# A hybrid S5, sliding-window and PEER block on one core: the table stages with all five engines in the order of the text

## The chip, the cores and the metric

The kernel runs on one core of a Trainium2 chip. The metric is the device time of one execution in microseconds. The core has TensorE (PE), VectorE (DVE), ScalarE (ACT) and GpSimd (POOL), and SyncE (SP), which issues loads. ScalarE issues DMAs too, in its own instruction order. Each engine works its instructions off in the order in which the program holds them and waits for others at semaphores, so that order is the thing that this change is about.

## The reference, cut

A decoder block of 512 tokens and width 1024: an S5 branch and a sliding-window attention branch, merged by gates, then the PEER mixer, a retrieval of single-neuron experts by product keys. All in float32. The mixer is the part that the change touches:

```python
def peer_mixer(xn, w_query, sub_keys, u_tab, v_tab):
    q = (xt @ w_query).reshape(t, PEER_HEADS, 2, PEER_KEY_DIM // 2)
    s = jnp.einsum('thkd,hknd->thkn', q, sub_keys)
    vals, idx = lax.top_k(s, PEER_TOPK)
    cand = vals[:, :, 0, :, None] + vals[:, :, 1, None, :]
    best, pos = lax.top_k(cand.reshape(t, PEER_HEADS, -1), PEER_TOPK)
    expert = i1 * N_SUB_KEYS + i2            # 8 heads x 16 of 16384 experts per token
    gate = jax.nn.softmax(best, axis=-1)
    def block_fn(args):
        a = jnp.einsum('cd,ced->ce', xb, u_tab[eb])
        w = gb * jax.nn.gelu(a, approximate=False)
        return jnp.einsum('ce,ced->cd', w, v_tab[eb])
```

## The kernel before

The first 128 tokens go through the mixer by gathering their experts' rows (`sparse`: an indirect load by GpSimd, L1192, and a multiply-add on VectorE, L1209 for a row of the u table and L1211 for one of the v table). The other 384 tokens go through it densely: all 16384 experts are multiplied, with a gate that is zero for those not chosen. The two tables are read in 128 units of 128 experts each.

A **u-unit** computes A = gelu(u . x) of its 128 experts for 384 tokens. Its table rows are loaded by SP (`t_raw`, L1124), split into a rounded part `hi` (ScalarE, L124) and the rest `lo` (VectorE, L125), and multiplied in 24 matmuls (L94 to L96, `pa`); ScalarE takes the gelu (L1136). The result stays on the chip (`A_first`, `A_mid`) or goes to DRAM by a store on ScalarE's queue (`u_g` to `A_d`, L1361). A **v-unit** loads its table rows (L1126), splits them likewise, loads A again if it was stored (`v_a`, L1345, SP) and the gates of eight units at a time (`v_g` from `G_d`, L1141, SP, in four parts), multiplies the two (`v_w`, VectorE L1149), splits the product into `v_wh` (ScalarE, L89) and `v_wl` (VectorE, L90) and adds 18 matmuls of 512 columns to the output (L1160, L1161, L1163, `po`).

The work runs in one list of 256 units, `order`: 96 u-units alone (**stage A**), then the other 32 u-units woven among the 128 v-units (**stage V**). In stage A a background generator, `early()`, is advanced by a credit per unit. It does the top-k (VectorE, L964 to L972, with number copies on ScalarE, L1004) and writes the gates as dense matrices: for each of 48 groups of 8 tokens VectorE builds two one-hot matrices and multiplies in the gates, ScalarE copies the first into another layout (`g_one`, L1108), TensorE multiplies the two (`pg`, L1092 and L1093) and ScalarE evicts the result in two pieces (`g_st`, L1095); every second group its queue stores them to DRAM (`G_d`, L1097). The product of a group is written in the text behind the next group's VectorE work:

```python
nc.vector.tensor_tensor(o1, self.iota16, wide(iT[:, 0, :]), op=ALU.is_equal)   # L1107, g_o
nc.scalar.copy(one, o1.rearrange("p b t -> p t b"))                            # L1108, g_one
nc.vector.tensor_tensor(ol, self.iota16, wide(iT[:, 1, :]), op=ALU.is_equal)   # L1109
nc.vector.tensor_mul(oh, ol, wide(gh))                                         # L1110, g_oh
nc.vector.tensor_mul(ol, ol, wide(gl))                                         # L1111, g_ol
if late:
    multiply(*late)                                                            # pg, g_st, G_d
late = (t1, one, oh, ol)
```

A step i of the loop under `manual_schedule` (L1328) writes, in this order: the table load of unit i+6 (five `t_raw` buffers), the split of unit i+2 (three `hi` and three `lo` buffers), in stage V the loads of `v_g` (five to eight ahead) and `v_a` (four ahead) and the preparation of `v_w` (two ahead); then the matmuls of unit i, with the gelu and the store of A; then the background work and some sparse rows. Engines named in `manual_schedule` keep that order of the text. The others are placed by a scheduler, which puts an instruction where it reckons that its operands are ready. Before, VectorE and GpSimd are named; TensorE, ScalarE and SP are placed by the scheduler. DMAs of SP and of ScalarE's queue share eight completion semaphores, given out in turn in the order of the schedule, and a DMA waits for the one before it on its semaphore.

Of the kernel before, what the change touches and what calls it, by code (L numbers as in the profile page):

```python
# [31 lines left out]
def run_some(gen, credit, add):  # L32

    credit += add
    while credit > 0:
        c = next(gen, None)
        if c is None:
            return 0.0
        credit -= c
    return credit  # L40
# [18 lines left out]
class Builder:  # L59
# [1155 lines left out]
    def run(self, out):  # L1215
        tc, nc, I, L = self.tc, self.nc, self.i, self.pool
        PS = bass.MemoryType.PSUM
        ET = mybir.EngineType
        NB, DT = 128, T - 128
        with ExitStack() as fs:  # L1220
# [104 lines left out]
            def ahead(i, n):  # L1325
                return order[i + n] if 0 <= i + n < len(order) else (2, 0)

            with tc.manual_schedule(engines={ET.DVE, ET.Pool}):  # L1328
                for i in range(-self.FAR, len(order)):
                    v, b = ahead(i, self.FAR)  # L1330
                    if v < 2:
                        raws[v, b] = self.table_load(v * NB + b)
                    if ahead(i, 2)[0] < 2:
                        parts[ahead(i, 2)] = self.unit_split(raws.pop(ahead(i, 2)))
                    if vp:
                        for part in range(self.PARTS):
                            v, b = ahead(i, 8 - part)
                            if v == 1 and b % self.GB == 0:
                                if part == 0:
                                    gg[b] = vp.tile([128, Gd.shape[0], self.GB, self.TS], F32, tag="v_g", name=self.nm("v_g"), bufs=2)  # L1340
                                self.g_load(gg[b], b, Gd, part)
                        v, b = ahead(i, 4)
                        if v == 1 and b not in as_:
                            as_[b] = vp.tile([128, DT], F32, tag="v_a", name=self.nm("v_a"), bufs=4)
                            nc.sync.dma_start(out=as_[b], in_=Ad[b])  # L1345
                        v, b = ahead(i, 2)
                        if v == 1:
                            ws[b] = self.w_prep(vp, as_.pop(b), gg[b - b % self.GB][:, :, b % self.GB, :])
                            if b in homes:
                                free.append(homes.pop(b))  # L1350
                    if i < 0:
                        continue
                    v, b = order[i]
                    if v == 0:
                        kept = bool(free)
                        dst = free.pop(0) if kept else self.wb.tile([128, DT], F32, tag="u_g", name=self.nm("u_g"), bufs=2)
                        self.a_mm(parts.pop((0, b)), xh[:, :, 128:], xl[:, :, 128:], dst)
                        if kept:
                            as_[b] = homes[b] = dst
                        else:  # L1360
                            nc.scalar.dma_start(out=Ad[b], in_=dst)  # L1361
                    else:
                        if b == NB - self.END:
                            for _ in sparse:
                                pass
                        if b == NB - 1:
                            fo = [self.wb.tile([128, D], F32, tag="raw", name=self.nm("fo"), bufs=self.WB[0])
                                  for j in range(DT // 128)]
                            for j, o in enumerate(fo):
                                nc.scalar.dma_start(out=o, in_=hd[j + 1])  # L1370
                        self.v_mm(parts.pop((1, b)), ws.pop(b), po, b == 0, b == NB - 1)
                    if not vp:
                        t_bg = run_some(bg, t_bg, self.RATE_A)
                        if i == self.ALONE - 10:
                            for _ in bg:
                                pass
                    if i >= 4 and self.ready:
                        t_sp = run_some(sparse, t_sp, self.RATE_V if vp else self.RATE_S)
                    if not vp and self.done:
                        rs.close()  # L1380
                        gs.close()
                        pv = L(fs, "pv", space=PS)
                        po = [[pv.tile([128, 512], F32, name=f"po{j}{i}") for i in range(2)] for j in range(DT // 128)]
                        vp = L(fs, "vp", side="right")
                for j in range(DT // 128):
                    for i in range(2):
                        c = slice(512 * i, 512 * i + 512)
                        nc.vector.tensor_add(fo[j][:, c], fo[j][:, c], po[j][i])
                        (nc.scalar if i else nc.sync).dma_start(out=out[j + 1][:, c], in_=fo[j][:, c])
# [77 lines left out]
```

## Time and profile before

| | |
|---|---|
| time, median of 3 runs | 1727.51 us (1727.5 to 1727.69) |
| the profiled execution | 1727.21 us |
| its span in the profile | 1725.4 us |
| mean granted TensorE clock | 0.983 |
| TensorE, VectorE, ScalarE, GpSimd busy | 1625.8, 1426.2, 844.4, 571.4 us |

Times in the profile are microseconds from the start of the span. Busy time is the time in which an engine worked on instructions; "idle before" is its idle time just ahead of an instruction, and the arrow behind it names what it waited for, found from semaphores. "issue" means that nothing was waited for that the profile shows. SPq and ACTq are the queues in which SP and ScalarE issue DMAs. A trailing x3 counts instructions that were put into one row. An instruction's row may begin a little ahead of the end of the one before it, since the engines overlap neighbours; a step is therefore read from start to start. The granted clock is TensorE's, as a share of full speed.

### The profile page before, as it was taken

How to read it: one execution, taken by the hardware profiler on the slowest of the kernel's cores; microseconds unless marked ns; L12 is line 12 of the kernel's file. 1: busy time of each engine (PE TensorE's matmuls, PEld its weight loads, DVE VectorE, ACT ScalarE, POOL GpSimd, SP SyncE). 2: the span in 40 equal slices, each digit the busy share in tenths (PEclk: the TensorE clock that was granted, in tenths of full speed). 3: DMA queues.
4: the chain of work that ended last, by engine and by line, in shares of the span. 5: the costliest groups of instructions: out<-in, count | busy, mean ns of one | idle time of the engine just before them, and what ended most of it. 6: DMA issues, size and time to landing. Idle time of an engine off the chain costs nothing.

```text
span 1725.4 us, 25152 instructions
## 1 busy us (share of the span) xinstructions
PE 1625.8 (94%) x8831; PEld 1429.5 (83%) x8831; DVE 1426.2 (83%) x2931; ACT 844.4 (49%) x1290; POOL 571.4 (33%) x472
## 2 busy tenths in 40 slices
PE   7789999998999899899899889999999999999998
PEld 5568877776899898898899888888888888888876
DVE  7799768897797999999999647877777777777876
ACT  5256565565564457667778423333333333333332
POOL 2563023332521232222222223334434343333441
PEclk9899999999999999999999989999999999999999
DMA  7823452656754567767678987889989989998874
GB/s 230 151 86 99 142 170 74 180 161 185 237 149 164 207 221 281 261 243 272 247 270 325 360 290 270 315 308 330 356 310 338 342 316 340 338 334 311 301 274 171
DMA packets 236302, 429.61 MB, mean 249 GB/s; under 512 B 17376, under 2 KB 153104, under 8 KB 233104
## 3 DMA queue, kind: packets, MB, share of 16 engines
q1 hardware_dynamic: 174464, 240.73, 42.4%
q0 software_dynamic: 36864, 134.23, 21.5%
q10 hardware_dynamic: 24848, 53.06, 9.5%
q8 instruction: 69, 1.13, 0.3%
q14 instruction: 57, 0.47, 0.1%
HBM read 373.69 MB, written 54.26 MB: 248 GB/s over the span
## 4 chain that ended last, share of the span: by engine, by line
PE 60%; DVE 18%; DMA 3%; ACT 3%; issue 3%; POOL 0%; SPq 0%; DVEq 0%; ACTq 0%; POOLq 0%
PE po L1160 10%; PE po L1161 10%; PE po L1163 10%; PE pa L94 7%; PE pa L96 7%; PE pa L95 6%; DVE lo L125 4%; DVE sp_row L1209 2%; ACT hi L124 1%; DVE g_oh L1110 1%; DVE t_s L966 1%; DMA gl<-g_d 1%; DVE g_o L1107 1%; DVE g_ol L1109 1%; DVE t_ix L968 1%
## 5 line engine op out<-in xcount | busy, mean ns | idle before, releaser
L124 ACT CAST hi<-t_raw 128x1024 fp32r<-128x1024 f32 x256 | 269.5, 1053 | 455.8 <-PE pa L95 192.8
L125 DVE TENSOR_TENSOR lo<-t_raw,hi 128x1024 fp32r<-128x1024 f32 x256 | 313.2, 1223 | 89.3 <-ACT hi L124 88.6
L94 PE MATMUL pa<-x2h,hi 128*128 128x384 f32 x1024 | 349.8, 342 | 26.7 <-ACT u_g L1136 24.5
L96 PE MATMUL pa<-x2h,lo 128*128 128x384 f32 x1024 | 350.0, 343 | 10.9 <-DVE lo L125 10.9
L95 PE MATMUL pa<-x2l,hi 128*128 128x384 f32 x1024 | 346.5, 338 | 0.0
L1192 POOL DMA_INDIRECT sp_row<-peer_u,sp_ei x128 | 188.4, 1472 | 417.7 <-DVE sp_row L1209 379.2
L1192 POOL DMA_INDIRECT sp_row<-peer_v,sp_ei x128 | 198.7, 1552 | 368.5 <-DVE sp_acc L1211 340.4
L1160 PE MATMUL po<-hi,v_wh 128*128 128x512 f32 x768 | 303.1, 395 | 3.2 <-ACT v_wh L89 3.2
L1161 PE MATMUL po<-lo,v_wh 128*128 128x512 f32 x768 | 302.7, 394 | 0.0
L1163 PE MATMUL po<-hi,v_wl 128*128 128x512 f32 x768 | 228.4, 394 | 0.0
L94 PEld LDWEIGHTS pa<-x2h,hi 128*128 128x128 f32 x1024 | 195.1, 191 | 33.6 <-ACT u_g L1136 27.8
L96 PEld LDWEIGHTS pa<-x2h,lo 128*128 128x128 f32 x1024 | 195.1, 191 | 16.5 <-DVE lo L125 15.7
L95 PEld LDWEIGHTS pa<-x2l,hi 128*128 128x128 f32 x1024 | 195.1, 191 | 1.5
L1160 PEld LDWEIGHTS po<-hi,v_wh 128*128 128x128 f32 x768 | 143.7, 187 | 37.6 <-ACT v_wh L89 4.1
L1163 PEld LDWEIGHTS po<-hi,v_wl 128*128 128x128 f32 x768 | 143.8, 187 | 35.4
L1161 PEld LDWEIGHTS po<-lo,v_wh 128*128 128x128 f32 x768 | 143.8, 187 | 33.3
L1211 DVE SCALAR_TENSOR_TENSOR sp_acc<-sp_row,sp_a,sp_acc 128x1024 f32<-128x1024 f32 x128 | 163.7, 1279 | 0.2
L1209 DVE SCALAR_TENSOR_TENSOR sp_row<-sp_row,xrow 128x1024 f32<-128x1024 f32 x128 | 155.7, 1217 | 5.4 <-DMA sp_row<-peer_u,sp_ei 5.4
L90 DVE TENSOR_TENSOR v_wl<-v_w,v_wh 128x384 fp32r<-128x384 f32 x128 | 71.5, 558 | 99.2 <-ACT v_wh L89 99.2
L89 ACT CAST v_wh<-v_w 128x384 fp32r<-128x384 f32 x128 | 65.5, 512 | 168.7 <-DVE v_w L1149 168.7
L124 ACT CAST hi<-raw 128x1024 fp32r<-128x1024 f32 x88 | 92.0, 1047 | 84.9 <-PE gps L95 15.5
L125 POOL TENSOR_TENSOR lo<-raw,hi 128x1024 fp32r<-128x1024 f32 x28 | 68.6, 2450 | 118.0 <-ACT hi L124 115.6
(455 smaller groups left out, 2999.4 us busy)
## 6 DMA issues: line engine op xcount, KB each, us to landing
t_raw<-peer_uT SPq DMA_DIRECT2D x128, 512.0 KB
t_raw<-peer_v SPq DMA_DIRECT2D x128, 512.0 KB
G_d<-g_st ACTq DMA_DIRECT2D x24, 1024.0 KB
v_g<-G_d SPq DMA_DIRECT2D x64, 384.0 KB
raw<-w_in SPq DMA_DIRECT2D x32, 512.0 KB
A_d<-u_g ACTq DMA_DIRECT2D x68, 192.0 KB
v_a<-A_d SPq DMA_DIRECT2D x68, 192.0 KB
raw<-w_ab SPq DMA_DIRECT2D x64, 128.0 KB
```

The costliest lines, as they stand in the source:

```text
L90: self.nc.vector.tensor_sub(lo, src, r32(hi))
L94: mm(out, lh, rh, start=first, stop=False)
L95: mm(out, lh, rl, start=False, stop=False)
L96: mm(out, ll, rh, start=False, stop=last)
L124: self.nc.scalar.copy(hi, raw)
L125: (self.nc.gpsimd if pool_lo else self.nc.vector).tensor_sub(lo, raw, r32(hi))
L1160: mm(po[j][i], wh[:, c], hi[:, hs[i]], start=first, stop=False)
L1161: mm(po[j][i], wh[:, c], lo[:, hs[i]], start=False, stop=False)
L1163: mm(po[j][i], wl[:, c], hi[:, hs[i]], start=False, stop=last)
L1192: nc.gpsimd.indirect_dma_start(out=got[k], out_offset=None, in_=self.i[n], in_offset=bass.IndirectOffsetOnAxis(ap=ei[:, s:s + 1], axis=0))
L1209: nc.vector.scalar_tensor_tensor(r, r, 1.0, xrow, op0=ALU.mult, op1=ALU.mult, accum_out=av[:, s:s + 1])
L1211: nc.vector.scalar_tensor_tensor(acc, r, av[:, s:s + 1], acc, op0=ALU.mult, op1=ALU.add)
```

## The change

One line: the set of engines that keep the order of the text under the loop of the 256 units has five members and not two.

```diff
-            with tc.manual_schedule(engines={ET.DVE, ET.Pool}):
+            with tc.manual_schedule(engines={ET.DVE, ET.Pool, ET.SP, ET.PE, ET.Activation}):
```

VectorE's and GpSimd's instructions in the table stages stand as before. ScalarE's order in stage A, before and after, at the same place (`hi` is the cast of a table unit; the gelu writes `u_g`; `g_one` and `g_st` belong to the gate groups). Before:

```order
636 L124 CAST hi_8837<-t_raw_8564 128x1024
637 L1136 ACTIVATE u_g_8765<-pa_8766 128x384
638 L1095 ACTIVATE g_st_8735<-pg_8736 128x128x4
639 L1095 ACTIVATE g_st_8735<-pg_8746 128x128x4
640 L1361 DMA A_d<-u_g_8765 128x384
641 L1108 COPY g_one_8728<-g_o_1603_8729 128x1024
642 L124 CAST hi_8904<-t_raw_8611 128x1024
643 L1136 ACTIVATE u_g_8841<-pa_8842 128x384
644 L1108 COPY g_one_8795<-g_o_1616_8796 128x1024
```

After, with the gelu of the same unit (`u_g_8765`) in the second row:

```order
638 L124 CAST hi_8761<-t_raw_8499 128x1024
639 L1136 ACTIVATE u_g_8765<-pa_8766 128x384
640 L1361 DMA A_d<-u_g_8765 128x384
641 L1108 COPY g_one_8795<-g_o_1616_8796 128x1024
642 L1095 ACTIVATE g_st_8735<-pg_8802 128x128x4
643 L1095 ACTIVATE g_st_8735<-pg_8812 128x128x4
644 L1097 DMA G_d<-g_st_8735 128x2048
645 L124 CAST hi_8837<-t_raw_8564 128x1024
646 L1136 ACTIVATE u_g_8841<-pa_8842 128x384
```

The cast `hi_8837` stood ahead of the gelu of `u_g_8765`; now it stands a unit later, behind `g_one_8795`, both evictions and the store. The group's copy stands a unit earlier against the gelus, and so do the evictions and, on TensorE, the matmuls `pg`, which now follow the matmuls of the same step's unit.

SP's order at the passage from stage A to stage V (table loads `t_raw`, gates `v_g`, stored A `v_a`). Before:

```order
245 L1124 DMA t_raw_11009<-peer_uT 128x1024
246 L1141 DMA v_g_11314<-G_d 128x6x128 x2
247 L1124 DMA t_raw_11046<-peer_uT 128x1024
248 L1141 DMA v_g_11314<-G_d 128x6x128 x2
249 L1141 DMA v_g_11692<-G_d 128x6x128 x2
250 L1124 DMA t_raw_11083<-peer_uT 128x1024
251 L1141 DMA v_g_11692<-G_d 128x6x128 x2
252 L1345 DMA v_a_12108<-A_d 128x384
253 L1345 DMA v_a_12140<-A_d 128x384
254 L1345 DMA v_a_12217<-A_d 128x384
255 L1345 DMA v_a_12494<-A_d 128x384
```

After:

```order
253 L1124 DMA t_raw_11268<-peer_uT 128x1024
254 L1124 DMA t_raw_11308<-peer_uT 128x1024
255 L1141 DMA v_g_11314<-G_d 128x6x128
256 L1124 DMA t_raw_11347<-peer_uT 128x1024
257 L1141 DMA v_g_11314<-G_d 128x6x128
258 L1126 DMA t_raw_11385<-peer_v 128x1024
259 L1141 DMA v_g_11314<-G_d 128x6x128
...
287 L1345 DMA v_a_12108<-A_d 128x384
```

The gate loads stood eight table loads earlier and four at a time, and four `v_a` loads stood right behind them; now one part stands behind each table load, and the first `v_a` load stands at row 287.

## Rows read from the trace of the kernel before

**Rows 1.** The page: busy us (share of the span) xinstructions, each engine.

```profile
PE 1625.8 (94%) x8831; PEld 1429.5 (83%) x8831; DVE 1426.2 (83%) x2931; ACT 844.4 (49%) x1290; POOL 571.4 (33%) x472
```

**Rows 2.** Two stretches: length, busy of PE, PEld, DVE, ACT, POOL, clock, DMA, GB/s.

```profile
700.00:725.00 25.00, 22.08 (x138) 21.13 (x138) 24.42 (x52) 19.15 (x21) 4.02 (x3) 0.86 0.73 268
1100.00:1125.00 25.00, 25.00 (x118) 21.34 (x117) 20.58 (x29) 9.76 (x14) 9.96 (x8) 1.00 0.79 284
```

**Rows 3.** Waits of DVE, 575 to 985 us: us in total, times, longest us.

```profile
DVE lo L125 <- ACT hi L124: 7.8, 6, 2.2
DVE g_ol L1109 <- PE pg L1093: 2.4, 2, 2.2
```

**Rows 4.** Timeline of DVE, 925 to 961: start, us, operation [idle before].

```profile
931.02 1.22 DVE L125 TENSOR_TENSOR lo<-t_raw,hi 128x1024 fp32r<-128x1024 f32 x1
932.16 0.69 DVE L1107 TENSOR_TENSOR g_o<-iota,g_iT 128x1024 f16<-128x1024 f16 x1
...
935.96 1.22 DVE L125 TENSOR_TENSOR lo<-t_raw,hi 128x1024 fp32r<-128x1024 f32 x1
...
951.11 1.22 DVE L125 TENSOR_TENSOR lo<-t_raw,hi 128x1024 fp32r<-128x1024 f32 x1
...
954.90 1.22 DVE L125 TENSOR_TENSOR lo<-t_raw,hi 128x1024 fp32r<-128x1024 f32 x1
...
959.77 1.23 DVE L125 TENSOR_TENSOR lo<-t_raw,hi 128x1024 fp32r<-128x1024 f32 x1 [0.17 <-ACT hi L124]
```

**Rows 5.** Timeline of DVE, 670 to 680 and 885 to 896.

```profile
672.10 1.22 DVE L125 TENSOR_TENSOR lo<-t_raw,hi 128x1024 fp32r<-128x1024 f32 x1
...
675.58 0.68 DVE L1107 TENSOR_TENSOR g_o<-iota,g_iT 128x1024 f16<-128x1024 f16 x1
...
678.23 1.22 DVE L125 TENSOR_TENSOR lo<-t_raw,hi 128x1024 fp32r<-128x1024 f32 x1
...
886.00 1.22 DVE L125 TENSOR_TENSOR lo<-t_raw,hi 128x1024 fp32r<-128x1024 f32 x1
...
893.65 1.22 DVE L125 TENSOR_TENSOR lo<-t_raw,hi 128x1024 fp32r<-128x1024 f32 x1
```

**Rows 6.** Timeline of ACT, 925 to 961.

```profile
926.49 0.59 ACT L1095 ACTIVATE g_st<-pg 128x512 f32<-128x512 f32 x1
...
927.45 2.06 ACT L1108 COPY g_one<-g_o 128x1024 f16<-128x1024 f16 x1
...
931.79 2.06 ACT L1108 COPY g_one<-g_o 128x1024 f16<-128x1024 f16 x1
...
933.74 1.08 ACT L1095 ACTIVATE g_st<-pg 128x512 f32<-128x512 f32 x2
...
944.30 1.11 ACT L1095 ACTIVATE g_st<-pg 128x512 f32<-128x512 f32 x2
...
945.81 2.17 ACT L1108 COPY g_one<-g_o 128x1024 f16<-128x1024 f16 x1 [0.40 <-ACT g_st L1095]
...
958.67 1.06 ACT L124 CAST hi<-t_raw 128x1024 fp32r<-128x1024 f32 x1 [0.62 <-PE pa L95]
```

**Rows 7.** Timeline of ACT, 975 to 1016.

```profile
980.61 1.04 ACT L124 CAST hi<-t_raw 128x1024 fp32r<-128x1024 f32 x1 [2.67 <-PE pa L95]
...
995.85 1.04 ACT L124 CAST hi<-t_raw 128x1024 fp32r<-128x1024 f32 x1 [13.81 <-DMA v_a<-A_d]
...
1010.21 1.05 ACT L124 CAST hi<-t_raw 128x1024 fp32r<-128x1024 f32 x1 [3.40 <-PE pa L95]
...
1014.37 1.05 ACT L124 CAST hi<-t_raw 128x1024 fp32r<-128x1024 f32 x1 [2.72 <-PE pa L95]
```

**Rows 8.** Timeline of SP, 970 to 990: DMA issues.

```profile
973.80 9.36 SPq L1141 DMA_DIRECT2D v_g<-G_d  x4
```

**Rows 9.** The chain that ended last, 984 to 996: start, us, what.

```profile
987.61 7.72 DMA v_a<-A_d
```

**Rows 10.** Waits of PE, 1640 to 1690: us in total, times, longest us.

```profile
PE po L1160 <- ACT v_wh L89: 3.2, 2, 1.6
```

## The prediction

> **What bounds the kernel now.** I read the busy shares of the engines first, then busy time by stretches, then the waits, and the timelines last, where a wait or a lack of one had to be priced. Over the whole program TensorE is the busy engine, VectorE is next, and ScalarE is busy for half of the time [rows 1]. That is a mean over stages with different limits. In stage A (96 u-units, with the top-k and gate work in the background; about 530 to 960 us) VectorE is busy 24.42 of 25 us and TensorE 22.08; in stage V (1010 us to the end) TensorE has 25.00 of 25 and VectorE 20.58 [rows 2]. The waits of VectorE from 575 to 985 us say the same: 7.8 us in all for ScalarE's `hi`, 2.4 us for TensorE's `pg`, and little else [rows 3]; most of the 7.8 us lies after 955 us, where the groups are done. So stage A runs at the rate at which VectorE gets through its own list, and the other engines fit themselves around it. VectorE's and GpSimd's order in these stages is already that of the text and stays so. The question is what the fixed order of ScalarE, TensorE and SP does to VectorE in stage A and to TensorE in stage V.
>
> **ScalarE in stage A, the loss.** Before, the `hi` of a unit stands ahead of the group's copy `g_one`, one unit further on than in the text; so when VectorE wants to make `lo`, its `hi` has long been there. After, the `hi` of the next unit stands behind `g_one` and both evictions `g_st` of the step. `g_one` waits for VectorE's `g_o` of the same step, and VectorE's next `lo` waits for that `hi`. This closes a ring over both engines, once per group step. Its price, piece by piece:
> - VectorE from the start of `lo` to the end of `g_o`: 932.16 + 0.69 - 931.02 = 1.83 us [rows 4].
> - `g_one`, start to the next start: 933.74 - 931.79 = 1.95 us. Two evictions without a store of G_d: 927.45 - 926.49 = 0.96; with one: 945.81 - 944.30 = 1.51 [rows 6].
> - `hi`, from its start to the start of the `lo` that waited for it: 959.77 - 958.67 = 1.10 us [rows 4, 6].
>
> The ring is thus 5.84 us without the store and 6.39 with it. VectorE's own time from `lo` to `lo` in a plain group step with one sparse row is 935.96 - 931.02 = 4.94 us, and without a sparse row 954.90 - 951.11 = 3.79 [rows 4]. Every step loses the ring less its own time, where that is positive. I went through the steps of stage A one by one, with VectorE's time from the trace and ScalarE's list from the new order (48 groups in all):
> - one sparse row, no store: 8 steps x 0.90 = 7.2 us; one sparse row, with store: 9 x 1.45 = 13.1 us;
> - no sparse row: 2 x 2.05 + 1 x 2.60 = 6.7 us;
> - two groups in one step: the ring is 1.83 + 1.95 + 0.96 + 1.95 + 1.51 + 1.10 = 9.30 against VectorE's own 893.65 - 886.00 = 7.65 [rows 5]; 3 x 1.65 = 5.0 us;
> - a group that stands behind top-k work in its step, so that `g_o` comes late: in the step shown `g_o` ends 675.58 + 0.68 - 672.10 = 4.16 us after `lo`, the ring is 8.17 and the own time 678.23 - 672.10 = 6.13 [rows 5], a loss of 2.04; ten such steps, between 0.5 and 2.7 us each: 14.1 us;
> - the other 12 groups have enough work of VectorE behind them (top-k, or no evictions yet): 0.3 us; steps without a group that hold one of the number copies: about 2 us.
>
> Together 48.3 us. VectorE's waits for `pg` go (2.4 us [rows 3]), because TensorE now does `pg` right behind the unit of its own step: **+46 us**. Bounds: at nothing, if ScalarE's list gets ahead by other slack that I haven't seen; and at about 60 us, if the evictions themselves come late because TensorE, with some 5.2 us of work in a step of 5.84 (rival 4), stands still in between. I take the sum, because every piece is a row of the same instructions.
>
> **The passage from stage A to V, a gain.** Before, SP has v_g and four v_a loads hoisted between the table loads. A v_g load can't start before the last stores of G_d: SP stands in four of them for 9.36 us at 973.80 [rows 8]. The v_a loads stand behind; the chain that ended last goes through one of them for 7.72 us at 987.61 [rows 9], and ScalarE's `hi` waits 13.81 us for it, since the store of A_d ahead of it on ScalarE shares a completion semaphore with that load [rows 7]. From the `hi` at 980.61 to that at 1014.37 there are four units in 33.76 us; a unit that is not held takes 1014.37 - 1010.21 = 4.16 us [rows 7], four 16.64. The loss is 17.1 us. After, each v_g part stands behind one table load more, from t_raw_11308 on, the first v_a load stands some 35 SP rows later, and the semaphores fall to other pairs: the A_d stores of these units share theirs with earlier stores and table loads. I count the whole as gone: **-17.1 us**. Bounds: -17.1 and 0, the second if the wait comes back for another load.
>
> **Stage V and the rest.** TensorE's two waits for `v_wh` near the end, 3.2 us [rows 10], come from places where ScalarE's order has two `hi` in a row ahead of `v_wh`; the text alternates them: **-3.2 us**. Otherwise TensorE is full there [rows 2], and its own order changes only within a unit: 0. The v_g and v_a loads, now just in time, are needed three units, 12.5 us, behind their issue (they stand right behind a table load, which is issued when the unit five before it has been split), against the 7.72 us of the slowest one that I have a row for: 0, up to +15 if some come late. Ahead of the table stages a few dozen VectorE rows change places: 0, +-3.
>
> **Sum**, on the profiled execution, 1727.2 us (span 1725.4; the median of three runs is 1727.51): 1727.2 + 46 - 17.1 - 3.2 = 1752.9, so **1753 us**, slower by 1.5%.
>
> **Rivals.**
> 1. ScalarE's half-empty time hides its order: it is busy 844.4 us of 1725.4 [rows 1], and may run on so far that its `hi` is never late; it holds three `hi` buffers. Then only the gains are left: 1727.2 - 17.1 - 3.2 = 1707 us. Against it: `g_one` can't start before `g_o` of its step, however idle ScalarE is, and the next `hi` stands behind it. Chance 0.13. The Trainium skill, Perfetto Trace Analysis, section "Identifying the Most-Contended Engine", tells to take the engine with the highest occupancy as the one that matters; read over the whole span this is TensorE, and the order of ScalarE at half its occupancy would be harmless, which is this rival. Read by stages, the rows disagree: the engine that is full in stage A is VectorE.
> 2. The passage keeps its stall in another form (an A_d store waits on a table load or a v_g load through the shared semaphore, and the `hi` behind it waits too): 1727.2 + 46 - 3.2 = 1770 us. It decides if such a load lands later than the unit allows. Chance 0.13.
> 3. The ring costs half: ScalarE gets to `g_one` late in some steps but catches up in those with top-k work, so 23 for 46: 1730 us, no change. Chance 0.07.
> 4. Slower on: the new short waits of TensorE in every group step lower its granted clock in stage A. A stretch at 0.86, between the full 2.4 GHz and the lower level of 1.2, is there before, with TensorE busy 22.08 of 25 us over four steps, 5.5 us each [rows 2]; a step at the full clock is some 5.2 us (an estimate: the unit's 4.16 us [rows 7] and the rest of those 5.5 for `pg`). At 1.2 GHz it would be 10.4, 4.5 us over the ring; three to seven such steps give 1766 to 1785 us. Chance 0.09.
>
> **How the numbers follow.** Likeliest, 0.58: 1753, by itself from 1743 to 1764. The rivals have 0.13, 0.13, 0.07 and 0.09. Leaving out the first rival and the tail of the last, the range is 1728 to 1776. About 0.2% is what a measurement of this kernel can tell from no change: faster 0.13, same 0.07, slower 0.80.
>
> **What would show it.** VectorE's waits for `hi` from 575 to 955 us, next to nothing before, come to some 45 us, 0.9 to 2.7 in a step; the starts of `lo` in plain group steps are 5.8 to 6.4 us apart, not 4.94; the wait of ScalarE for v_a at 982 us and those of TensorE for `v_wh` are gone; stage V is as long as before. The prediction is wrong if VectorE stays at 24 of 25 us in stage A (rival 1), if `hi` waits for a load in the passage (rival 2), or if stage V gets longer by waits for v_g, v_a or `v_wh`.

## The result and the profile after

The changed kernel takes 1749.24 us (median of four runs, 1748.38 to 1752.06) against 1727.51. The ratio of the two, taken from the means of the runs and not from the medians, is 1.0131, with a 95% interval of 1.0113 to 1.0148. It is slower, and the forecast was 1753. The profiled execution took 1752.06 us, the highest of the four, with a span of 1750.3; the sum had been made against the profiled execution of before and gave 1752.9.

To see where the time went I cut both traces at the same instructions: the starts of the 4th, 83rd, 98th and 256th table cast `lo` on VectorE, whose order the change leaves alone. (These are the casts meant wherever a cast is counted below.) The 4th begins stage A's steady part, the 83rd comes after the last gate group, the 98th after the passage, the 256th is the last.

| stretch, us | before | after | difference | forecast |
|---|---|---|---|---|
| start to 4th cast | 536.6 | 538.9 | +2.3 | 0 +-3 |
| 4th to 83rd: stage A | 423.2 | 470.6 | +47.5 | +46 |
| 83rd to 98th: the passage | 80.7 | 62.7 | -17.9 | -17.1 |
| 98th to 256th: stage V | 668.8 | 661.7 | -7.1 | -3.2 |
| 256th to the end | 16.2 | 16.3 | +0.1 | 0 |

The waits of VectorE from 575 to 1010 us, where before there were 7.8 us for `hi` and 2.4 for `pg` [rows 3]: us in total, times, longest.

```profile
DVE lo L125 <- ACT hi L124: 49.0, 39, 2.8
```

Nothing else is left in that view, and the one wait is the forecast one. The timeline of VectorE at the third token tile, the last 128 of the 384 dense tokens, whose gate groups stand closest together (start, us, operation, idle before), to be held against [rows 4]:

```profile
955.54 1.23 DVE L125 TENSOR_TENSOR lo<-t_raw,hi 128x1024 fp32r<-128x1024 f32 x1 [0.79 <-ACT hi L124]
...
961.92 1.23 DVE L125 TENSOR_TENSOR lo<-t_raw,hi 128x1024 fp32r<-128x1024 f32 x1 [1.35 <-ACT hi L124]
963.06 0.68 DVE L1107 TENSOR_TENSOR g_o<-iota,g_iT 128x1024 f16<-128x1024 f16 x1
...
967.76 1.23 DVE L125 TENSOR_TENSOR lo<-t_raw,hi 128x1024 fp32r<-128x1024 f32 x1 [1.96 <-ACT hi L124]
...
974.13 1.23 DVE L125 TENSOR_TENSOR lo<-t_raw,hi 128x1024 fp32r<-128x1024 f32 x1 [1.29 <-ACT hi L124]
```

And that of ScalarE in the same time, which answers to [rows 6]:

```profile
957.40 2.04 ACT L1108 COPY g_one<-g_o 128x1024 f16<-128x1024 f16 x1 [1.50 <-DVE g_o L1107]
959.36 1.08 ACT L1095 ACTIVATE g_st<-pg 128x512 f32<-128x512 f32 x2
960.47 0.33 ACTq L1097 DMA_DIRECT2D G_d<-g_st  x1
960.84 1.05 ACT L124 CAST hi<-t_raw 128x1024 fp32r<-128x1024 f32 x1 [0.40 <-ACT g_st L1095]
...
963.78 2.04 ACT L1108 COPY g_one<-g_o 128x1024 f16<-128x1024 f16 x1 [1.50 <-DVE g_o L1107]
965.71 1.09 ACT L1095 ACTIVATE g_st<-pg 128x512 f32<-128x512 f32 x2
966.68 1.05 ACT L124 CAST hi<-t_raw 128x1024 fp32r<-128x1024 f32 x1
```

One turn of the ring can be read off: `lo` starts at 955.54, `g_one` waits for `g_o` and starts at 957.40, the evictions and the store follow, `hi` starts at 960.84 and the next `lo` at 961.92. That is 6.38 us with a store; the next turn, without one, is 967.76 - 961.92 = 5.84. The forecast pieces gave 6.39 and 5.84. Both engines wait for each other once per turn, ScalarE 1.50 us for `g_o` and VectorE 0.79 to 1.96 for `hi`, and neither is full. By windows the same (length, busy of PE, PEld, DVE, ACT and POOL, granted clock, DMA share, GB/s), against [rows 2]:

```profile
943.00:968.00 25.00, 22.96 (x176) 22.27 (x174) 18.97 (x26) 18.18 (x22) 3.56 (x4) 1.00 0.81 283
1150.00:1175.00 25.00, 25.00 (x115) 20.88 (x114) 19.87 (x25) 8.90 (x13) 8.03 (x7) 1.00 0.80 283
```

No engine is busy all the time in the first, in the gate groups; TensorE is in the second, in stage V. In the passage ScalarE's long wait [rows 7] is gone, and SP issues thirteen table loads without a load of another kind between them where it had stood in the `v_g` loads [rows 8]:

```profile
1016.84 1.05 ACT L124 CAST hi<-t_raw 128x1024 fp32r<-128x1024 f32 x1 [0.45 <-ACT u_g L1136]
...
1021.00 1.05 ACT L124 CAST hi<-t_raw 128x1024 fp32r<-128x1024 f32 x1 [0.45 <-ACT u_g L1136]
```

```profile
990.57 53.90 SPq L1124 DMA_DIRECT2D t_raw<-peer_uT  x13
```

The units follow at 1021.00 - 1016.84 = 4.16 us, the rate of a unit that is not held.

### The profile page after: what moved, and what is told of

Same layout as the page of the kernel before. It is cut to its first block, busy times and chain, and to the rows that moved or that the text cites. A ratio compares the mean times of both kernels' runs of the same rounds, so it can differ in the third digit from the quotient of the medians.

```text
span 1750.3 us, 25058 instructions
## 1 busy us (share of the span) xinstructions
PE 1632.7 (93%) x8831; PEld 1442.4 (82%) x8831; DVE 1429.7 (82%) x2931; ACT 849.5 (49%) x1290; POOL 536.7 (31%) x472
## 4 chain that ended last, share of the span: by engine, by line
PE 52%; DVE 21%; ACT 6%; issue 5%; DMA 3%; SPq 0%; POOL 0%; ACTq 0%; DVEq 0%; POOLq 0%
PE po L1161 10%; PE po L1160 10%; PE po L1163 10%; DVE lo L125 6%; PE pa L96 5%; PE pa L94 5%; PE pa L95 5%; ACT hi L124 2%; ACT g_st L1095 2%; DVE sp_row L1209 2%; DVE g_o L1107 1%; DVE t_s L966 1%; ACT g_one L1108 1%; DMA gl<-g_d 1%; DVE t_ix L968 1%
## 5 line engine op out<-in xcount | busy, mean ns | idle before, releaser
L94 PE MATMUL pa<-x2h,hi 128*128 128x384 f32 x1024 | 354.8, 347 | 1.7 <-ACT u_g L1136 1.6
L95 PE MATMUL pa<-x2l,hi 128*128 128x384 f32 x1024 | 350.2, 342 | 0.0
L1192 POOL DMA_INDIRECT sp_row<-peer_u,sp_ei x128 | 169.0, 1320 | 453.8 <-DVE sp_row L1209 412.1
L1192 POOL DMA_INDIRECT sp_row<-peer_v,sp_ei x128 | 183.6, 1434 | 387.9 <-DVE sp_acc L1211 358.7
L1163 PE MATMUL po<-hi,v_wl 128*128 128x512 f32 x768 | 241.0, 394 | 0.0
L1163 PEld LDWEIGHTS po<-hi,v_wl 128*128 128x128 f32 x768 | 143.6, 187 | 35.6
L1108 ACT COPY g_one<-g_o 128x1024 f16<-128x1024 f16 x48 | 98.3, 2047 | 94.2 <-DVE g_o L1107 89.2
```

What stands on the lines that cost most here:

```text
L94: mm(out, lh, rh, start=first, stop=False)
L95: mm(out, lh, rl, start=False, stop=False)
L1163: mm(po[j][i], wl[:, c], hi[:, hs[i]], start=False, stop=last)
L1192: nc.gpsimd.indirect_dma_start(out=got[k], out_offset=None, in_=self.i[n], in_offset=bass.IndirectOffsetOnAxis(ap=ei[:, s:s + 1], axis=0))
```

## The experiments

The table holds the same stretches for all nine kernels, from their profiled executions; the medians are of all their runs. The ratios go by runs of the kernel before that were timed along with each (medians 1727.54 to 1728.62 us), and by all of these runs, not by the medians.

| kernel | median, us | ratio to before, 95% interval | to 4th | stage A | passage | stage V | end |
|---|---|---|---|---|---|---|---|
| only ScalarE added | 1759.84 | 1.0182 (1.0165 to 1.0199) | 536.8 | 469.5 | 71.4 | 662.0 | 18.1 |
| only SP added | 1712.02 | 0.9906 (0.9889 to 0.9922) | 536.1 | 423.3 | 63.5 | 670.6 | 16.2 |
| all but ScalarE | 1728.72 | 1.0002 (0.9992 to 1.0012) | 536.3 | 443.6 | 62.4 | 668.6 | 14.4 |
| all, `hi` ahead | 1719.85 | 0.9948 (0.9931 to 0.9964) | 539.6 | 438.3 | 62.5 | 662.0 | 16.3 |
| `hi` ahead, TensorE free | 1707.65 | 0.9882 (0.9865 to 0.9898) | 535.8 | 429.8 | 59.7 | 661.9 | 18.1 |
| `hi` and one unit ahead | 1708.73 | 0.9888 (0.9872 to 0.9905) | 535.2 | 431.4 | 61.5 | 662.0 | 16.3 |
| `hi` and two units ahead | 1779.59 | 1.0294 (1.0276 to 1.0311) | 536.5 | 504.5 | 59.2 | 662.0 | 16.3 |
| `hi` behind `g_one` | 1721.06 | 0.9961 (0.9947 to 0.9975) | 535.8 | 442.7 | 62.5 | 662.0 | 16.3 |
| by stage | 1707.15 | 0.9882 (0.9866 to 0.9899) | 536.6 | 423.5 | 63.5 | 664.7 | 16.2 |

**Only ScalarE.** Is the ring ScalarE's order alone?

```diff
-            with tc.manual_schedule(engines={ET.DVE, ET.Pool, ET.SP, ET.PE, ET.Activation}):
+            with tc.manual_schedule(engines={ET.DVE, ET.Pool, ET.Activation}):
```

> Of the three engines that the change adds to the set only ScalarE is added; TensorE and SP stay with the scheduler. Theory (the ring of hi behind g_one and the evictions is ScalarE's order alone): from the 4th to the 83rd table cast on VectorE some 470 us as in the changed kernel (423 before), with VectorE waiting about 49 us for hi; the passage keeps its stall, because SP still hoists v_g and v_a, and the waits for v_wh are gone: 1727 + 47 - 6 = 1768 us. Rival (the ring needs TensorE's and SP's order too): stage A stays at 423 us, 1721 us.

Stage A takes 469.5 us, as with all five, so ScalarE's order alone closes the ring. The passage keeps a stall, but a smaller one than I had expected (71.4 us, where 80.7 was before), and so the time is 1760 and not 1768. Its rows are instructive. SP stands in the hoisted loads again, and ScalarE's `hi` waits again, this time for a `v_g` load and not for a `v_a` load:

```profile
1009.91 16.61 SPq L1141 DMA_DIRECT2D v_g<-G_d  x6
```

```profile
1030.36 0.33 ACTq L1361 DMA_DIRECT2D A_d<-u_g  x1
1030.78 1.04 ACT L124 CAST hi<-t_raw 128x1024 fp32r<-128x1024 f32 x1 [14.21 <-DMA v_g<-G_d]
```

The semaphores in the two traces agree with that. Here the store at 1030.36 us waits for, and then uses, the semaphore of the `v_g` load that SP issued at 1022.63 us and that landed at 1030.28; before, the store ahead of the `hi` at 995.85 us used that of the `v_a` load issued at 987.61 [rows 9]. So the load that the store of A stands behind differs between these kernels; that one of the hoisted loads is on its semaphore is enough.

**Only SP.** Does SP's order alone remove the stall of the passage?

```diff
+            with tc.manual_schedule(engines={ET.DVE, ET.Pool, ET.SP}):
```

> Of the three only SP is added. Theory (the passage's stall comes from the hoisted v_g and v_a loads): the stall is gone, no wait of ScalarE for v_a, the stretch from the 83rd to the 98th cast takes 63 us and not 81; stage A and the two waits for v_wh are as before: 1709 to 1711 us. Rival (the stall comes back on a table load or on the order of ScalarE's stores): 1727 us.

The passage takes 63.5 us and stage A what it took before; 1712.02 us is a microsecond over what was expected, since stage V is 1.8 us longer than before (670.6 against 668.8). This one engine is a gain of 0.9%.

**All but ScalarE.** Do SP and TensorE keep that gain?

```diff
+            with tc.manual_schedule(engines={ET.DVE, ET.Pool, ET.SP, ET.PE}):
```

> SP and TensorE are added, ScalarE stays with the scheduler. Theory: gain of the passage without the ring, and VectorE's 2.4 us of waits for pg gone: 1707 to 1710 us. Rival (TensorE's order, pg right behind its unit, costs something by itself): over 1712 us, with waits of TensorE for g_one.

They don't: 1728.72 us, on the rival's side and well above its 1712. TensorE's order is the only difference to the kernel with only SP added, and it costs 20.3 us in stage A (443.6 against 423.3). Part of it is one place, where VectorE stands 4.13 and 5.07 us at the start of the third token tile (`g_gs` is its first work on that tile's gates):

```profile
884.98 1.23 DVE L125 TENSOR_TENSOR lo<-t_raw,hi 128x1024 fp32r<-128x1024 f32 x1 [4.13 <-ACT hi L124]
891.27 0.29 DVE L1076 TENSOR_SCALAR g_gs<-gtr 128x128 f32<-128x128 f32 x1 [5.07 <-ACT g_iT L1071]
```

The rest comes in steps of some 5.3 us in the groups of that tile. What makes them is the subject of the next four runs. So a term of my sum was wrong, though the sum was right: I had given TensorE's order in stage A a gain of 2.4 us and no cost.

**All five, `hi` ahead of the groups.** The text itself is changed, so that ScalarE's cast of the next unit stands ahead of the background work and the ring isn't closed. VectorE's order stays.

```diff
-                        parts[ahead(i, 2)] = self.unit_split(raws.pop(ahead(i, 2)))
+                        parts[ahead(i, 2)] = rest(ahead(i, 2))      # lo; hi too, if it isn't there
...
                     if not vp:
+                        cast(ahead(i, 3))                            # hi alone, on ScalarE
                         t_bg = run_some(bg, t_bg, self.RATE_A)
```

> All five engines keep the order of the text, as in the changed kernel, but the text of stage A has the hi of unit i+3 ahead of the background work of step i (ahead of g_one and the evictions), and its lo where it was. Theory (the loss is the place of hi alone): VectorE's waits for hi in stage A are gone, 423 us or less from the 4th to the 83rd cast, and the gains of the passage and of v_wh stay: 1702 us. Rival (the loss lies in the fixed order of TensorE or of the evictions): 1740 to 1750 us.

The ring is gone: from 575 to 900 us VectorE waits 0.6 us for `hi`. But the time is 1720 and not 1702. VectorE waits again at the end, in the 13 steps of the third tile whose groups stand close together (timeline of VectorE):

```profile
930.03 1.22 DVE L1336 TENSOR_TENSOR lo<-t_raw,hi 128x1024 fp32r<-128x1024 f32 x1 [0.19 <-ACT hi L1329]
...
935.39 1.23 DVE L1336 TENSOR_TENSOR lo<-t_raw,hi 128x1024 fp32r<-128x1024 f32 x1 [1.48 <-ACT hi L1329]
...
940.62 1.22 DVE L1336 TENSOR_TENSOR lo<-t_raw,hi 128x1024 fp32r<-128x1024 f32 x1 [0.15 <-ACT hi L1329]
...
945.96 1.22 DVE L1336 TENSOR_TENSOR lo<-t_raw,hi 128x1024 fp32r<-128x1024 f32 x1 [0.31 <-ACT hi L1329]
```

From start to start these steps are 5.2 to 5.4 us: they are TensorE's steps, a unit of 4.16 us and the `pg` of a group. TensorE itself has one wait from 908 to 985 us, of 2.9 us. The loss must lie ahead of it. The waits of TensorE from 560 to 908 us, here:

```profile
PE pg L1092 <- ACT g_one L1108: 21.9, 12, 3.8
PE pa L96 <- DVE lo L1336: 8.4, 8, 3.3
PE pg L1092 <- DVE g_ol L1111: 5.7, 2, 3.8
PE pa L94 <- ACT u_g L1136: 0.6, 1, 0.6
```

and in the kernel with only SP added:

```profile
PE pa L94 <- ACT u_g L1136: 10.8, 11, 2.8
PE pa L96 <- DVE lo L125: 8.9, 12, 1.5
PE pg L1092 <- ACT g_one L1108: 3.5, 5, 1.8
PE pa L94 <- ACT A_mid L1136: 1.2, 2, 1.0
PE pa L94 <- ACT A_first L1136: 1.0, 1, 1.0
PE pg L1092 <- DVE t_bv L964: 0.8, 1, 0.8
```

Together 36.6 us with `hi` ahead and 26.2 with only SP. In the order of the text TensorE stands at `pg` until `g_one` comes, with a unit behind it that could run. In the scheduler's order `pg` comes a unit or two later and TensorE is ahead when the close groups begin; it may then fall behind VectorE for a while without holding it. That was a theory at this point, and the next three runs test it.

**TensorE back to the scheduler, `hi` ahead.**

```diff
+            with tc.manual_schedule(engines={ET.DVE, ET.Pool, ET.SP, ET.Activation}):
```

> As the kernel with hi ahead of the background work (1720 us), but TensorE goes back to the scheduler; ScalarE and SP keep the order of the text. Theory (the fixed order of TensorE costs 12 to 15 us by itself, by taking away the units that TensorE was ahead when the groups of the third token tile came, at 5.3 us of TensorE work a step): from the 4th to the 83rd cast 423 to 425 us and not 438: 1704 to 1707 us. Rival (what is left over 423 us lies in ScalarE's order or the table loads): 1718 to 1721 us.

1707.65 us; stage A 429.8 us, which is 8.5 less, though not the 423 to 425 expected. TensorE's order did cost most of what was missing. A part of the rest is only the place of the cut: stage A and passage together take 489.5 us here and 486.8 with only SP added, since the passage is 3.8 us shorter (59.7 against 63.5).

**One unit ahead, in the order of the text.** The matmuls of unit i+1 stand ahead of the background work of step i, the gelu where it was.

```diff
                         cast(ahead(i, 3))
+                        mm_u(ahead(i, 1))          # the 24 matmuls; mm_u does a unit once
```

> As the kernel with hi ahead (1720 us), all five engines in the order of the text, but the text puts the matmuls of unit i+1 ahead of the background work of step i; the gelu stays at its place. Theory (the lost lead of TensorE): one unit more of lead gives back up to 4 us, 1716 us. Rival (TensorE is held by waits for g_one, whatever its lead): 1720 us.

1708.73 us, with all five engines in the order of the text. Stage A loses 6.9 us (438.3 to 431.4), more than the 4 expected; TensorE's waits for `g_one` from 575 to 1000 us fall from 24.8 to 5.3 us. Another 4.4 us lie ahead of the table stages (539.6 and 535.2 us to the 4th cast), where the texts of the two are the same; that stretch varies from 535.2 to 539.6 over the kernels here, and why is open.

The lead can also be read off the traces, as the time from the start of a unit's `lo` to the start of the last of its 24 matmuls, at the 71st and the 76th unit, among the close groups:

| kernel | 71st unit, us | 76th unit, us |
|---|---|---|
| only SP added | 6.70 | 9.53 |
| all but ScalarE | 14.15 | 14.60 |
| all, `hi` ahead | 14.04 | 13.47 |
| `hi` ahead, TensorE free | 7.15 | 9.15 |
| `hi` and one unit ahead | 10.04 | 10.67 |

The rows for the 71st unit, with only SP added and with `hi` ahead:

```profile
902.07 1.22 DVE L125 TENSOR_TENSOR lo<-t_raw,hi 128x1024 fp32r<-128x1024 f32 x1
908.77 0.33 PE L96 MATMUL pa<-x2h,lo 128*128 128x384 f32 x1
```

```profile
908.35 1.23 DVE L1336 TENSOR_TENSOR lo<-t_raw,hi 128x1024 fp32r<-128x1024 f32 x1 [1.21 <-ACT hi L1329]
922.39 0.34 PE L96 MATMUL pa<-x2h,lo 128*128 128x384 f32 x1
```

TensorE is some 14 us behind in the two slow kernels and stays there, and VectorE, with three buffers of `hi` and of `lo`, is held to its pace: the five steps between the two units take 27.0 us with `hi` ahead. With only SP added TensorE is 6.7 us behind, falls back to 9.5, and the same five steps take 23.6 us. So the lost lead is shown. What took it isn't separated: TensorE waits longer in the slow kernels, and its granted clock is lower there as well, from the 4th to the 83rd cast 0.95 in "all but ScalarE" and 0.96 with `hi` ahead, against 0.99 with only SP added and 0.98 in the two kernels that give the lead back. At the lower level of 1.2 GHz a matmul of 384 columns follows the one before after 0.32 us, at 2.4 GHz after 0.17 (the kernel with one unit ahead, from 892.4 and from 896 us), so that some of the lag is the clock's.

**Two units ahead.**

```diff
                         cast(ahead(i, 3))
+                        for n in range(1, 3):
+                            mm_u(ahead(i, n))
```

> As the last, with the matmuls of units i+1 and i+2 ahead of the background work of step i. Theory of the lost lead: up to 8 us back, 1712 us, unless VectorE begins to wait for pg, which comes later. Rival: 1720 us.

A miss of 68 us, on the wrong side. What I had named as a condition came true, and by far. The waits of VectorE from 560 to 1040 us, and those of TensorE:

```profile
DVE g_ol L1109 <- PE pg L1093: 38.1, 19, 4.0
DVE lo L1336 <- ACT hi L1329: 20.7, 13, 4.1
DVE g_gs L1076 <- ACT g_iT L1071: 16.2, 3, 8.2
```

```profile
PE pa L94 <- ACT u_g L1376: 59.0, 40, 4.1
PE pa L96 <- DVE lo L1336: 19.3, 13, 3.6
PE pa L94 <- ACT A_mid L1376: 12.3, 8, 3.5
```

TensorE now waits for the gelu to free one of two `pa` buffers, ahead of a `pg` for which VectorE waits in turn, since `g_ol` has two buffers. The lead has an optimum at one unit here. That more buffers would move it wasn't tried.

**`hi` behind `g_one`, ahead of the evictions.** Is the ring the sum of its pieces?

```diff
             nc.scalar.copy(one, o1.rearrange("p b t -> p t b"))
+            self.hook()                            # cast(ahead(i, 3)), if not yet done
```

> All five engines in the order of the text; the hi of unit i+3 stands behind g_one, but ahead of the two evictions and the store of G_d. The ring is then 1.83 + 1.95 + 1.10 = 4.88 us, below the 4.94 of a step with a sparse row and below TensorE's 5.3. Theory (the ring is the sum of its pieces): only the steps with nothing behind g_o lose, two by 1.1 us, and those with a number copy: 1720 to 1724 us, as with hi ahead of g_one. Rival (the wait for g_o is what counts, the evictions were hidden): 1740 to 1750 us.

1721.06 us: with the evictions out of the ring it is 4.88 us by the sum, too short to be seen over TensorE's steps. Stage A is 442.7 us, 28 less than in the changed kernel and 4.4 more than with `hi` ahead of everything.

**By stage.** SP keeps the order of the text throughout, ScalarE and TensorE only from unit 96 on.

```diff
+            two = {ET.DVE, ET.Pool, ET.SP}
+            for engines, steps in ((two, range(-self.FAR, self.ALONE)),
+                                   (two | {ET.PE, ET.Activation}, range(self.ALONE, len(order)))):
+                with tc.manual_schedule(engines=engines):
+                    for i in steps:
```

> VectorE, GpSimd and SP keep the order of the text throughout; TensorE and ScalarE are the scheduler's in stage A and keep the order of the text only from unit 96 on. Theory: stage A as before (423 us from the 4th to the 83rd cast), the passage's gain of 17 to 18 us from SP, and the 6 us of the two v_wh places from ScalarE's order in stage V: 1704 to 1706 us. Rival (what the order of one stage gains, the join of the two gives back): 1709 us or more.

1707.15 us, 1.15 over the upper end of what was expected, and below the rival's 1709; stage A 423.5 us, as before the change, the passage 63.5, and stage V 5.9 us shorter than with only SP added. With the two kernels at 1708 us it is the fastest here, 1.2% under the kernel before, and the three can't be told apart by their intervals.

## Why the prediction was right, point by point

The mechanisms of the two large terms were right, and so were their sizes. That the sum for the profiled execution came out at 1752.9 against 1752.06 us is partly luck: the parts were off by +2.3, +1.5, -0.8, -3.9 and +0.1 us, which cancel.

- **The ring on VectorE and ScalarE** (+46): right in place, mechanism and size, 5.84 and 6.38 us a turn against 5.84 and 6.39, 49.0 us of waits, +47.5 us in stage A; half of it, the third rival, is out. That ScalarE alone makes it, and that the evictions are a part of it, is shown by the runs with only ScalarE and with `hi` behind `g_one`.
- **The first rival** (ScalarE's half-empty time hides its order) is out: ScalarE is busy for 18.18 of 25 us in the close groups after the change, idle in the rest, and VectorE waits for it in every turn. By the Trainium skill, Perfetto Trace Analysis, section "Identifying the Most-Contended Engine", the engine with the highest occupancy is the one to work on first, with TensorE judged by its weight loads. The trace of after has a stretch in which the limit is a ring and no engine is full (TensorE's weight loads 22.27, VectorE 18.97, ScalarE 18.18 of 25 us), and occupancy doesn't point at it.
- **The passage** (-17.1): right, -17.9. SP's order alone does it. The part of the semaphores is as argued: with the loads hoisted, as in the kernel with only ScalarE added, the stall comes back on the one that shares the store's semaphore, which is the second rival's mechanism.
- **Stage V** (-3.2): right in sign, half the size (the list of signs, with "stage V is as long as before", left the term out). From the 98th cast to the end before took 685.0 us, the changed kernel 678.0, "only ScalarE" 680.1 and "all but ScalarE" 683.0. So ScalarE's order gave 4.9 us and that of TensorE (with SP's) 2.0. The term for `v_wh` was mis-sized because I took the idle time of the two waits [rows 10] for their whole cost: by the starts of TensorE's units, the unit ahead of each wait is 5.95 us long, the one behind it 4.31 and the others around them 4.20, so each place costs 1.86 us and both 3.7. Most of the other 1.2 us of ScalarE's part is not in the v-units at all: with only ScalarE added the first of them starts 6.1 us behind the 98th cast and not 7.2. I had put TensorE's order at 0, "only within a unit"; but within the last unit it finishes the first output earlier (the scheduler puts all six matmuls of L1163 last), and the final additions on VectorE, which wait 5.66 us for it before, wait 3.80 in "all but ScalarE".
- **TensorE's order in stage A** (-2.4 and no cost): this step failed without showing. Its true price, 8 to 20 us in the kernels without the ring, was covered: the ring's turn of 5.84 us or more is longer than TensorE's step of 5.3, and stage A takes 469.5 us with ScalarE's order alone and 470.6 with TensorE's and SP's as well. The waits for `pg` did go, as the step said. Had the ring not been there, rival 1 would have come out at about 1720 and not 1707, as the kernel with `hi` ahead shows.
- **The slower clock** (rival 4): its condition came, its price did not. TensorE's waits for `g_one` grow from 1.7 us to 49.6 us, and its granted clock falls from 0.98 to 0.94 in stage A as a whole. But in the stretch of the close groups shown above it is 1.00, the full 2.4 GHz, and from 575 us on VectorE never waits for `hi` longer than 2.8 us, where the rival had 4.5 over the ring in a step. Nor does the rival's step of 5.2 us follow from its rows: 4.16 and the rest of 5.5 make 5.5 again. The steps measured later, 5.2 to 5.4 us, are near it all the same. Stage A from the 4th to the 83rd cast, before and after, with the columns of [rows 2]:

```profile
536.59:959.77 423.18, 395.56 (x2647) 378.72 (x2646) 408.31 (x1084) 274.39 (x319) 105.83 (x64) 0.98 0.72 256
538.90:1009.55 470.65, 408.71 (x2661) 396.73 (x2660) 411.41 (x1083) 278.08 (x321) 84.34 (x65) 0.94 0.67 236
```

## What to carry to other kernels

An engine that is half idle can still set the pace if its instructions wait, in a fixed order, for the engine that waits for it: add up one turn of the ring from start to start and compare it with the fullest engine's own step. A program order is a lead as well: work that stands behind a wait can't be done early, and the lead that an engine has when a dense stretch begins is worth its time there (here 6.9 and 8.5 us of stage A). Costs that are covered by a longer ring don't show in the sum and come up once the ring is gone, so try the parts of such a change one by one: here one engine of three was a gain of 0.9% and the whole a loss of 1.3%.

## What the runs showed of the hardware

In the kernel with only ScalarE added, the issue of a store on ScalarE's queue held up the cast behind it for 14.21 us, until a load that SP had issued, with no data in common with it, had landed. In the kernel before the change it was 13.81 us for another load. In both traces the store waits for, and then uses, the semaphore that this load counts up. The issue of a DMA is thus a place where an engine can wait for a load of another queue.
